# The last token blocks of an encoder layer get an order of their own, and every reciprocal root a third-order step

## The chip, the cores and the metric

The kernel runs on one core of one Trainium2 chip. The core has a matrix engine (TensorE, PE in the profile), a vector engine (VectorE, DVE), an activation engine (ScalarE, ACT), GpSimd (POOL) and a queue engine (SyncE, SP) that issues nearly all transfers between HBM and on-chip memory. Each engine carries out its instructions in the order in which they were written into its stream, and they wait for each other on semaphores. The metric is the device time of one execution in microseconds, lower is better.

## The reference, cut to what matters

One encoder layer is computed for two independent sequences of 512 tokens, `x_prompt` and `x_sample`, with 1024 channels:

```python
def rms_norm(x, g):
    xf = x.astype(jnp.float32)
    y = xf * lax.rsqrt(jnp.mean(xf * xf, axis=-1, keepdims=True) + EPS)
    return (y * g.astype(jnp.float32)).astype(x.dtype)

def swiglu(x, w_gate, w_up, w_down):
    return (jax.nn.silu(x @ w_gate) * (x @ w_up)) @ w_down

# encoder_layer: D_MODEL 1024, D_FF 2816
    x = x + 0.5 * swiglu(rms_norm(x, ffn1_norm), ffn1_w_gate, ffn1_w_up, ffn1_w_down)
    ...   # attention and a bidirectional mLSTM, side by side, merged and projected
    x = x + 0.5 * swiglu(rms_norm(x, ffn2_norm), ffn2_w_gate, ffn2_w_up, ffn2_w_down)
# trunk
    return rms_norm(x, final_norm)
```

The change touches the very end: the last additions into `x`, and the final `rms_norm`, which needs for each token the sum of squares over all 1024 channels before any of its channels can be scaled and stored. It also touches the reciprocal square root that every normalization in the layer uses.

## The kernel before, in words

**Stages.** The first feed-forward runs for both sequences together (profile lines L282 and L523), then the mixing stage (attention and mLSTM) once for each sequence (L678, L906, L932, L1013 and others), then the second feed-forward for both together, again L282 and L523. Each fp32 product is made of three matmuls on a high and a low part of the operands.

**The down projection.** `ffn_down` forms its 2x2 block product (two sequences by two halves of the channels) out of seven block products instead of eight; `DOWN` names them in the order in which they run, ending with T4, T1, B22. The 2816 hidden channels are taken in four chunks, so there are 28 steps, and the last seven finish the outputs. A step gives four token blocks of 128 tokens (`d` or `b`, 0 to 3), each a 128x512 tile in one PSUM bank. `flush_` adds the finished bank to its accumulator (L540). In the last seven steps it then calls `done(s, h, b)`: sequence `s`, half `h` of the channels, token block `b`. T4 finishes (0,1), T1 finishes (1,1), and B22, the last product of all, finishes (1,0). T1 and B22 use the same four banks (three named mm, one named pso), so B22's matmuls on a bank wait until T1's addition has read it.

**After each block.** `done2` squares the finished half on ScalarE with a running sum (`square`, L1152), and multiplies it in place by half of `final_norm` (L1338): on GpSimd, or on VectorE for (1,0). Once all halves of a group of token blocks are there (four blocks for sequence 0; blocks 0 and 1, then 2 and 3, for sequence 1), `row_scale` (L1161) adds the two half sums and runs `rstd_cols`, a chain of twelve small VectorE instructions (L157 to L168) that computes the reciprocal root from an integer first guess and three Newton steps. Then each block of 128x1024 is scaled by its root on ScalarE (L1352; the last block of sequence 1 on VectorE, L1350), and SP stores it with one 512 KB transfer (L1353).

**The order.** A planner orders each engine's instructions from the program's order, its priorities and its own estimate of costs. An instruction passed through `pin` (`tc.keep_in_program_order`) keeps its place in the program's order. In `done2` nothing is pinned. `rstd_cols` is used by 21 chains over the whole kernel, so an instruction more or less in it can change the planner's order elsewhere. Its small tiles come from a pool with five buffers for each width.

Of the kernel before, what the change touches and what calls it, by code (L numbers as in the profile page):

```python
# [16 lines left out]
P = 128  # L17
S = 512
D = 1024
# [3 lines left out]
EPS = 1e-6  # L23
# [3 lines left out]
def encoder(ctx, tc, I, outs):  # L27
    nc = tc.nc
# [5 lines left out]
    spool = ctx.enter_context(tc.tile_pool(name="spool", bufs=4))  # L34
# [7 lines left out]
    def nm(s):  # L42
        n_id[0] += 1
        return f"{s}_{n_id[0]}"
# [98 lines left out]
    def emit_hl(src, g, k, xh, xl):  # L143
# [2 lines left out]
                                       op0=ALU.mult, op1=ALU.subtract)  # L146
        return i1, i2

    def rstd_cols(v, width, n):


        def t_(dt=F32):
            w = max(width, 4)
            return spool.tile([P, w], dt, tag=f"rs{w}", bufs=5, name=nm("rs"))[:, 0:width]
        V = nc.vector
        a = t_()
        V.tensor_scalar(a, v, 1.0 / n, EPS, op0=ALU.mult, op1=ALU.add)  # L157
        b = t_(I32)
        V.tensor_scalar(b, a.bitcast(I32), 1, None, op0=ALU.logical_shift_right)
        y_ = t_(I32)  # L160
        V.tensor_scalar(y_, b, -1.0, 1597463007.0, op0=ALU.mult, op1=ALU.add)
        y = y_.bitcast(F32)
        for _ in range(3):
            t = t_()
            V.scalar_tensor_tensor(t, y, -0.5, y, op0=ALU.mult, op1=ALU.mult)
            V.tensor_tensor(t, t, a, op=ALU.mult)
            r = t_()
            V.scalar_tensor_tensor(r, t, 1.5, y, op0=ALU.add, op1=ALU.mult)  # L168
            y = r
        return y  # L170

    def col_sums(acc, bs=(0, 1, 2, 3)):
        p = PT()
# [42 lines left out]
    V_ = nc.vector  # L216
    G_ = nc.gpsimd
    HK_ = KD // 2

    B11, B21, B22, T4, T1, T2_, T3 = range(7)  # L220
# [215 lines left out]
    DH = KD // 2  # L436
    n_steps = len(DOWN) * len(CHUNKS)

    def ffn_down(wd, rb, ring, tail, xres, done, at_step, hook):
# [91 lines left out]
        def flush_(i, d, p):  # L531
            m, last = DOWN[i % 7], i >= n - 7
            acc = {B11: e16[:, d], T2_: e16[:, DH + d], T1: e5[:, d], B21: xs[0][:, d], T4: xs[0][:, DH + d],
                   T3: xs[1][:, DH + d], B22: xs[1][:, d]}[m]
            if last and m == T1:
                acc = xs[1][:, DH + d]
            if i < 7 and m in (B11, T2_, T1):
                nc.scalar.activation(acc, p, AF.Copy, scale=0.5)
            else:
                V_.scalar_tensor_tensor(acc, p, 0.5, acc, op0=ALU.mult, op1=ALU.add)  # L540
# [616 lines left out]
    def row_scale(sq, n=slice(0, 4)):  # L1157

        w = n.stop - n.start
        t = spool.tile([P, 4], F32, tag="cs4", bufs=4, name=nm("rsum"))[:, 0:w]  # L1160
        V_.tensor_tensor(t, sq[:, 0, n], sq[:, 1, n], op=ALU.add)  # L1161
        return rstd_cols(t, w, D)
# [86 lines left out]
    nhl = [None, None]  # L1249
    ssq1, ssq2, ssq3 = [[sums_tile() for _ in range(2)] for _ in range(3)]  # L1250

    def done1(s, h, b):
# [75 lines left out]
    fn = []  # L1328
# [3 lines left out]
        for half in range(2):  # L1332
            nc.gpsimd.dma_start(fn[half], I["final_norm"][half * S:(half + 1) * S].partition_broadcast(P))

    def done2(s, h, b):
        x_ = xs[s][:, h * 4 + b, :]
        square(x_, ssq3[s][:, h, b:b + 1])
        (V_ if (s, h) == (1, 0) else G_).tensor_tensor(x_, x_, fn[h], op=ALU.mult)  # L1338
        if s == 0 and h == 1 and b == 3:
            n = slice(0, 4)  # L1340
        elif s == 1 and h == 0 and b % 2:
            n = slice(b - 1, b + 1)
        else:
            return
        r = row_scale(ssq3[s], n)
        for i in range(n.start, n.stop):
            v = xs[s].rearrange("p (h b) c -> p h b c", h=2)[:, :, i, :]
            r_ = r[:, i - n.start:i - n.start + 1]
            if s and i == 3:
                V_.tensor_scalar(v, v, r_, None, op0=ALU.mult)  # L1350
            else:
                nc.scalar.activation(v, v, AF.Copy, scale=r_)  # L1352
            nc.sync.dma_start(outs[s][0, i * P:(i + 1) * P, :].rearrange("p (h c) -> p h c", h=2), v)  # L1353

    ffn_down(I["ffn2_w_down"][0], rbuf[1], up.ring, tail, lambda s, h: x2buf[s][:, h], done2, n_steps - 14, load_fn)


def host_consts():
# [39 lines left out]
```

## Time and profile before

| quantity | value |
|---|---|
| time, median of three runs | 2130.68 us (2130.02 to 2132.34) |
| time of the profiled execution | 2131.81 us |
| its span, first to last instruction | 2130.0 us |
| TensorE matmul busy | 2071.1 us, 97% of the span |
| VectorE busy | 1579.5 us, 74% |
| ScalarE busy | 968.5 us, 45% |
| GpSimd busy | 104.1 us, 5% |
| mean granted TensorE clock | 0.997 |

The profile is of one execution. Its rows give a start in microseconds from the span's start, a duration, the engine, the line of the kernel, the operation and the tiles; a bracket at the end names the idle time just ahead of an instruction and what ended it. A row with a count above 1 merges instructions that follow each other, and its duration is theirs together. VectorE and ScalarE let an independent instruction begin a little before the one ahead has ended, so start-to-start distances are shorter than durations.

### The profile page before, as it was taken

How to read it: one execution, taken by the hardware profiler on the slowest of the kernel's cores; microseconds unless marked ns; L12 is line 12 of the kernel's file. 1: busy time of each engine (PE TensorE's matmuls, PEld its weight loads, DVE VectorE, ACT ScalarE, POOL GpSimd, SP SyncE). 2: the span in 40 equal slices, each digit the busy share in tenths (PEclk: the TensorE clock that was granted, in tenths of full speed). 3: DMA queues.
4: the chain of work that ended last, by engine and by line, in shares of the span. 5: the costliest groups of instructions: out<-in, count | busy, mean ns of one | idle time of the engine just before them, and what ended most of it. 6: DMA issues, size and time to landing. Idle time of an engine off the chain costs nothing.

```text
span 2130.0 us, 26826 instructions
## 1 busy us (share of the span) xinstructions
PE 2071.1 (97%) x9472; PEld 1689.2 (79%) x9472; DVE 1579.5 (74%) x2817; ACT 968.5 (45%) x1739; POOL 104.1 (5%) x110
## 2 busy tenths in 40 slices
PE   6999999999999999999999999999999999999997
PEld 5877788888888777878887887788877778888885
DVE  7888887776696796574668755754978887786686
ACT  6534444442225466454435654544644444442223
POOL 1000000001000110100102001010000000000002
PEclk9999999999999999999999999999999999999998
DMA  8465554389765222333352232454464654479753
GB/s 266 150 197 186 182 196 142 131 303 378 281 219 162 78 71 64 95 103 97 117 159 81 60 90 79 129 178 158 154 197 159 197 165 166 142 261 386 284 207 122
DMA packets 294486, 361.81 MB, mean 170 GB/s; under 512 B 17776, under 2 KB 187776, under 8 KB 293328
## 3 DMA queue, kind: packets, MB, share of 16 engines
q1 hardware_dynamic: 293760, 358.84, 50.6%
q0 software_dynamic: 592, 1.27, 0.3%
q8 instruction: 74, 1.21, 0.2%
q14 instruction: 60, 0.49, 0.1%
HBM read 255.15 MB, written 104.89 MB: 169 GB/s over the span
## 4 chain that ended last, share of the span: by engine, by line
PE 74%; DVE 10%; DMA 6%; issue 6%; ACT 4%; POOL 0%; SPq 0%; DVEq 0%; ACTq 0%; POOLq 0%
PE mm L678 14%; PE pss L282 13%; PE pst L282 8%; PE mm L523 8%; PE mm L282 7%; PE pss L523 4%; PE pst L523 4%; PE mm L662 3%; PE pso L523 3%; DMA rbuf<-t 2%; DMA wr<-in_ffn_w_up_dram 2%; PE pso L932 1%; PE mm L1106 1%; PE pso L1062 1%; DVE w L241 1%
## 5 line engine op out<-in xcount | busy, mean ns | idle before, releaser
L678 PE MATMUL mm<-xh,w 128*128 128x512 f32 x896 | 292.0, 395 | 0.0
L282 PE MATMUL pss<-xc,w 128*128 128x512 f32 x1056 | 258.4, 391 | 12.4 <-DVE t L311 12.4
L282 PE MATMUL mm<-xc,w 128*128 128x512 f32 x1056 | 256.0, 391 | 2.5 <-ACT f L291 2.4
L282 PE MATMUL pst<-xc,w 128*128 128x512 f32 x1056 | 255.4, 390 | 0.0
L282 PEld LDWEIGHTS pss<-xc,w 128*128 128x128 f32 x1056 | 196.6, 188 | 60.4 <-DVE t L311 20.0
L282 PEld LDWEIGHTS mm<-xc,w 128*128 128x128 f32 x1056 | 196.8, 188 | 46.8 <-ACT f L291 6.6
L282 PEld LDWEIGHTS pst<-xc,w 128*128 128x128 f32 x1056 | 197.3, 188 | 43.2 <-ACT t L315 2.5
L203 DVE TENSOR_TENSOR w<-wr,w 128x1024 fp32r<-128x1024 f32 (+1 forms) x112 | 135.9, 1215 | 106.0 <-ACT w L202 100.7
L678 PEld LDWEIGHTS mm<-xh,w 128*128 128x128 f32 x896 | 167.6, 188 | 32.1
L523 PE MATMUL mm<-w,rt 128*128 128x512 f32 x792 | 185.6, 390 | 1.1 <-DMA rt<-rbuf 1.1
L678 PE MATMUL mm<-xl,w 128*128 128x512 f32 x448 | 176.7, 394 | 0.0
L523 PEld LDWEIGHTS mm<-w,rt 128*128 128x128 f32 x792 | 148.4, 188 | 32.5 <-DMA rt<-rbuf 1.8
L240 ACT ACTIVATE w<-t 128x512 fp32r<-128x512 f32 x176 | 107.0, 628 | 122.8 <-DVE t L266 42.0
L202 ACT ACTIVATE w<-wr 128x1024 fp32r<-128x1024 f32 (+1 forms) x112 | 114.4, 1028 | 99.4 <-PE mm L678 29.4
L241 DVE TENSOR_TENSOR w<-t,w 128x512 fp32r<-128x512 f32 x176 | 118.0, 689 | 44.5 <-ACT w L240 41.5
L282 PE MATMUL pss<-xc,f 128*128 128x512 f32 x528 | 128.4, 392 | 0.0
L282 PEld LDWEIGHTS pss<-xc,f 128*128 128x128 f32 x528 | 98.2, 188 | 23.6 <-DVE t L319 3.6
L580 ACT ACTIVATE w<-wr 128x512 fp32r<-128x512 f32 x72 | 44.6, 631 | 132.4 <-PE pso L523 64.3
L580 ACT ACTIVATE w<-t 128x512 fp32r<-128x512 f32 x82 | 51.6, 632 | 115.9 <-PE pst L523 47.3
L678 PEld LDWEIGHTS mm<-xl,w 128*128 128x128 f32 x448 | 84.3, 188 | 15.7
L523 PE MATMUL pss<-w,rt 128*128 128x512 f32 x396 | 94.0, 389 | 0.0
L523 PE MATMUL pst<-w,rt 128*128 128x512 f32 x396 | 93.7, 389 | 0.0
(316 smaller groups left out, 3644.4 us busy)
## 6 DMA issues: line engine op xcount, KB each, us to landing
rt<-rbuf SPq DMA_DIRECT2D x154, 512.0 KB, 5.8
wr<-in_w_in_dram SPq DMA_DIRECT2D x72, 512.0 KB, 3.6
wr<-in_ffn_w_gate_dram SPq DMA_DIRECT2D x56, 512.0 KB, 5.3
rbuf<-tab SPq DMA_DIRECT2D x90, 256.0 KB, 3.2
wr<-in_ffn_w_up_dram SPq DMA_DIRECT2D x44, 512.0 KB, 4.2
rbuf<-t SPq DMA_DIRECT2D x88, 256.0 KB, 3.5
rbuf<-f SPq DMA_DIRECT2D x66, 256.0 KB, 3.2
rbuf<-R SPq DMA_DIRECT2D x64, 256.0 KB, 3.5
```

Of the source, the lines that this page charges most:

```text
L202: pin(nc.scalar.activation(hi, raw, AF.Copy))
L203: pin(lo_eng.tensor_tensor(lo, raw, f(hi), op=ALU.subtract))
L240: pin(nc.scalar.activation(t[:, 0], src, AF.Copy))
L241: pin(V_.tensor_tensor(t[:, 1], src, f(t[:, 0]), op=ALU.subtract))
L282: nc.tensor.matmul(p, a[:, k, :], xt[:, b, k, :], start=(first and k == 0 and i == 0), stop=(k == HK_ - 1 and i == 2), skip_group_check=True)
L523: nc.tensor.matmul(p, r[:, b, d * P:(d + 1) * P], u[:, a, :], start=(first and q == 0 and k == 0), stop=(q == len(us) - 1 and k == 2), ski ...
L580: nc.scalar.activation(hi, src, AF.Copy)
L662: nc.tensor.matmul(p[b][:, :N], a[:, k, bs], w_[:, kl, :], start=(k == 0 and i == 0), stop=(k == KD - 1 and i == 2))
L678: nc.tensor.matmul(p, a[:, k, :], b, start=(k == 0 and i == 0), stop=(k == n - 1 and i == 2))
L932: nc.tensor.matmul(po, Vst[:, kv_, hk, :], w, start=(kv_ == 0 and i == 0), stop=(kv_ == 3 and i == 1))
L1062: nc.tensor.matmul(po, vm[:, a, t, hs_], b, start=(t == 0 and n == 0), stop=(t == 3 and n == 2))
L1106: nc.tensor.matmul(p[b], a[:, k, bs], w_[:, k - k0, :], start=(k == 0 and i == 0), stop=(k == KD - 1 and i == 2))
```

## The change

**The root.** `rstd_cols` is split: it forms `a = v/n + EPS`, and the new `rstd_of` does the rest, with the integer guess, one Newton step (three instructions), and one step of third order (five instructions). That is eleven instructions where there were twelve, and five small tiles a chain. It applies to every normalization of the kernel.

**T1 of sequence 1, half 1.** The product with `final_norm` moves from GpSimd to VectorE and is written to `e5`, which is free by then. After block 3 one VectorE instruction forms `half_ms` (`hm`), the half's sum of squares over 1024 plus EPS.

**B22, half 0.** `flush_` hands the block to `ends2`, all of whose instructions are pinned. Blocks 0 to 2: addition (VectorE), square (ScalarE), product with `final_norm` into `e16` (VectorE). After block 1 comes the root chain of blocks 0 and 1 (`last_scale(0)`), after block 2 the scaling of block 0 on ScalarE, each half by itself, each with a store of its own (256 KB). Block 3 is added in two column halves of 256; the first is squared on ScalarE, the second on VectorE, and that partial sum goes into `hm`. Then block 1 is scaled and stored by halves; then the chain of blocks 2 and 3 runs; then block 3's half 0 is scaled and multiplied by `final_norm` in one VectorE instruction, its half 1 on ScalarE, block 2's half 1 on VectorE and its half 0 on ScalarE, with four stores. Sequence 0 keeps its way.

```diff
+    def rs_tile(width, dt=F32):
+        w = max(width, 4)
+        return spool.tile([P, w], dt, tag=f"rs{w}", bufs=5, name=nm("rs"))[:, 0:width]
+
+    def rstd_of(a, width, pin=lambda i: i):
+
+        V = nc.vector
+        t_ = lambda dt=F32: rs_tile(width, dt)
+        b = t_(I32)
+        pin(V.tensor_scalar(b, a.bitcast(I32), 1, None, op0=ALU.logical_shift_right))
+        y_ = t_(I32)
+        pin(V.tensor_scalar(y_, b, -1.0, 1597463007.0, op0=ALU.mult, op1=ALU.add))
+        y = y_.bitcast(F32)
+        t = t_()
+        pin(V.scalar_tensor_tensor(t, y, -0.5, y, op0=ALU.mult, op1=ALU.mult))
+        pin(V.tensor_tensor(t, t, a, op=ALU.mult))
+        pin(V.scalar_tensor_tensor(t, t, 1.5, y, op0=ALU.add, op1=ALU.mult))
+        y, t, p, q = t, y, b.bitcast(F32), t_()
+        pin(V.tensor_tensor(t, y, y, op=ALU.mult))
+        pin(V.tensor_tensor(t, t, a, op=ALU.mult))
+        pin(V.tensor_scalar(p, t, 0.375, -1.25, op0=ALU.mult, op1=ALU.add))
+        pin(V.tensor_tensor(p, p, t, op=ALU.mult))
+        pin(V.scalar_tensor_tensor(q, p, 1.875, y, op0=ALU.add, op1=ALU.mult))
+        return q
+
     def rstd_cols(v, width, n):
-        for _ in range(3):
-            t = t_()
-            V.scalar_tensor_tensor(t, y, -0.5, y, op0=ALU.mult, op1=ALU.mult)
-            V.tensor_tensor(t, t, a, op=ALU.mult)
-            r = t_()
-            V.scalar_tensor_tensor(r, t, 1.5, y, op0=ALU.add, op1=ALU.mult)
-            y = r
-        return y
+        a = rs_tile(width)
+        nc.vector.tensor_scalar(a, v, 1.0 / n, EPS, op0=ALU.mult, op1=ALU.add)
+        return rstd_of(a, width)
...
             if last and m == T1:
                 acc = xs[1][:, DH + d]
+            if last and m == B22 and ends:
+                ends(d, p, acc, e16, e5)
+                return
...
-                done(1, 1, d)
+                done(1, 1, d, e5)
...
-    def done2(s, h, b):
+    half_ms = [None]
+
+    def store(s, i, h, v):
+        return nc.sync.dma_start(outs[s][0, i * P:(i + 1) * P, h * S:(h + 1) * S], v)
+
+    def done2(s, h, b, spare=None):
         x_ = xs[s][:, h * 4 + b, :]
         square(x_, ssq3[s][:, h, b:b + 1])
-        (V_ if (s, h) == (1, 0) else G_).tensor_tensor(x_, x_, fn[h], op=ALU.mult)
...
+        if s:
+            V_.tensor_tensor(spare[:, b], x_, fn[1], op=ALU.mult)
+            if b == 3:
+                t = half_ms[0] = spool.tile([P, 4], F32, tag="cs4", bufs=4, name=nm("hm"))
+                V_.tensor_scalar(t, ssq3[1][:, 1], 1.0 / D, EPS, op0=ALU.mult, op1=ALU.add)
             return
+        G_.tensor_tensor(x_, x_, fn[h], op=ALU.mult)
...
+    def last_scale(b0):
+
+        a = rs_tile(2)
+        sq, hm = ssq3[1][:, 0, b0:b0 + 2], half_ms[0][:, b0:b0 + 2]
+        pin(V_.scalar_tensor_tensor(a, sq, 1.0 / D, hm, op0=ALU.mult, op1=ALU.add))
+        return rstd_of(a, 2, pin)
+
+    first_r = []
+
+    def ends2(b, p, acc, pre0, pre1):
+
+        H = S // 2
+        ssq, hm = ssq3[1][:, 0, b:b + 1], half_ms[0][:, 3:4]
+        junk = T2(F32, "f2")
+
+        def on_act(i, h, r):
+            v = (pre0, pre1)[h][:, i]
+            pin(nc.scalar.activation(v, v, AF.Copy, scale=r))
+            pin(store(1, i, h, v))
+
+        if b < 3:
+            pin(V_.scalar_tensor_tensor(acc, p, 0.5, acc, op0=ALU.mult, op1=ALU.add))
+            pin(nc.scalar.activation(junk, acc, AF.Square, accum_out=ssq))
+            pin(V_.tensor_tensor(pre0[:, b], acc, fn[0], op=ALU.mult))
+            if b == 1:
+                first_r.append(last_scale(0))
+            if b == 2:
+                for h in range(2):
+                    on_act(0, h, first_r[0][:, 0:1])
+            return
+        for c in (slice(0, H), slice(H, S)):
+            pin(V_.scalar_tensor_tensor(acc[:, c], p[:, c], 0.5, acc[:, c], op0=ALU.mult, op1=ALU.add))
+            if c.start == 0:
+                pin(nc.scalar.activation(junk[:, c], acc[:, c], AF.Square, accum_out=ssq))
+        more = spool.tile([P, 4], F32, tag="cs4", bufs=4, name=nm("more"))[:, 0:1]
+        pin(V_.scalar_tensor_tensor(junk[:, H:], acc[:, H:], 1.0, acc[:, H:], op0=ALU.mult, op1=ALU.mult, accum_out=more))
+        pin(V_.scalar_tensor_tensor(hm, more, 1.0 / D, hm, op0=ALU.mult, op1=ALU.add))
+        for h in range(2):
+            on_act(1, h, first_r[0][:, 1:2])
+        r = last_scale(2)
+        pin(V_.scalar_tensor_tensor(acc, acc, r[:, 1:2], fn[0], op0=ALU.mult, op1=ALU.mult))
+        on_act(3, 1, r[:, 1:2])
+        pin(store(1, 3, 0, acc))
+        pin(V_.tensor_scalar(pre1[:, 2], pre1[:, 2], r[:, 0:1], None, op0=ALU.mult))
+        pin(store(1, 2, 1, pre1[:, 2]))
+        on_act(2, 0, r[:, 0:1])
```

More of the change, by code (lines that the diff above doesn't have):

```diff
@@ L437, in encoder, with ffn_down @@
     n_steps = len(DOWN) * len(CHUNKS)
-    def ffn_down(wd, rb, ring, tail, xres, done, at_step, hook):
+    def ffn_down(wd, rb, ring, tail, xres, done, at_step, hook, ends=None):
         n = n_steps
@@ L1355, in encoder @@
[L1355 removed]
+        if s:
[3 more added lines that the diff above has]
+                V_.tensor_scalar(t, ssq3[1][:, 1], 1.0 / D, EPS, op0=ALU.mult, op1=ALU.add)
+            return
+        G_.tensor_tensor(x_, x_, fn[h], op=ALU.mult)
+        if h == 0 or b < 3:
+            return
@@ new lines, in done2 @@
+        r = row_scale(ssq3[s])
+        for i in range(4):
+            v = xs[s].rearrange("p (h b) c -> p h b c", h=2)[:, :, i, :]
+            nc.scalar.activation(v, v, AF.Copy, scale=r[:, i:i + 1])
+            nc.sync.dma_start(outs[s][0, i * P:(i + 1) * P, :].rearrange("p (h c) -> p h c", h=2), v)
+    def last_scale(b0):
[3 more added lines that the diff above has]
+        return rstd_of(a, 2, pin)
@@ L1358, in host_consts @@
+    ffn_down(I["ffn2_w_down"][0], rbuf[1], up.ring, tail, lambda s, h: x2buf[s][:, h], done2, n_steps - 14, load_fn,
+             ends2)
 def host_consts():
```

26 lines of the change are left out of this document (2 added, 24 removed).

## The prediction

> **What bounds the kernel now.** I read the page's busy table first, then TensorE's waits over the whole span.
>
> ```profile
> PE 2071.1 (97%) x9472; PEld 1689.2 (79%) x9472; DVE 1579.5 (74%) x2817; ACT 968.5 (45%) x1739; POOL 104.1 (5%) x110
> PE pss L1147 <- DVE raw L1195: 13.7, 2, 11.3
> PE pst L848 <- DVE t L581: 4.4, 4, 1.8
> PE pst L185 <- DVE rs L168: 1.7, 4, 0.5
> ```
>
> TensorE is the bound: it idles for 2130.0 - 2071.1 = 58.9 us. What the change can win lies in that idle time, and most of it at two places, the first 16 us and the end. So the end comes next, in the timeline:
>
> ```profile
> 2100.86 1.16 DVE L157 TENSOR_SCALAR rs<-rsum 128x4 f32<-128x4 f32 x1
> 2102.06 0.17 DVE L159 TENSOR_SCALAR rs<-rs 128x4 int32<-128x4 int32 x1
> 2102.26 0.17 DVE L161 TENSOR_SCALAR rs<-rs 128x4 int32<-128x4 int32 x1
> 2102.34 0.69 DVE L540 SCALAR_TENSOR_TENSOR xs<-mm,xs 128x512 f32<-128x512 f32 x1
> 2104.11 1.14 DVE L165 SCALAR_TENSOR_TENSOR rs<-rs 128x4 f32<-128x4 f32 x1
> 2105.48 0.16 DVE L168 SCALAR_TENSOR_TENSOR rs<-rs,rs 128x4 f32<-128x4 f32 x1
> 2105.74 4.28 ACT L1352 ACTIVATE xs<-xs,rs 128x1024 f32<-128x1024 f32 x4 [1.90 <-DVE rs L168]
> 2107.08 6.28 PE L523 MATMUL mm<-w,rt 128*128 128x512 f32 x27
> 2109.32 0.69 DVE L540 SCALAR_TENSOR_TENSOR xs<-mm,xs 128x512 f32<-128x512 f32 x1 [1.35 <-PE mm L523]
> 2109.92 0.61 ACT L1152 ACTIVATE f<-xs 128x512 f32<-128x512 f32 x1
> 2110.53 0.61 ACT L1152 ACTIVATE f<-xs 128x512 f32<-128x512 f32 x1
> 2111.05 0.19 ACT L1152 ACTIVATION_READ_ACCUMULATOR f<-xs 128x1 f32 x1
> 2112.49 1.29 DVE L1338 TENSOR_TENSOR xs<-xs,tab 128x512 f32<-128x512 f32 x1 [2.48 <-ACT f L1152]
> 2113.20 2.20 PE L523 MATMUL pso<-w,rt 128*128 128x512 f32 x9
> 2118.26 0.69 DVE L540 SCALAR_TENSOR_TENSOR xs<-pso,xs 128x512 f32<-128x512 f32 x1
> 2120.40 0.15 DVE L1161 TENSOR_TENSOR rsum<-sqs 128x2 f32<-128x2 f32 x1
> 2122.84 0.16 DVE L168 SCALAR_TENSOR_TENSOR rs<-rs,rs 128x2 f32<-128x2 f32 x1
> 2123.10 1.15 ACT L1352 ACTIVATE xs<-xs,rs 128x1024 f32<-128x1024 f32 x1 [1.02 <-DVE rs L168]
> 2123.11 0.75 DVE L1350 TENSOR_SCALAR xs<-xs,rs 128x1024 f32<-128x1024 f32 x1
> 2124.27 1.20 SPq L1353 DMA_DIRECT2D out_dram<-xs  x2
> 2122.00:2122.50 0.50, 0.00 (x0) 0.00 (x0) 0.36 (x3) 0.08 (x1) 0.00 (x0) 0.50 0.44 172
> 2128.00:2128.50 0.50, 0.00 (x0) 0.00 (x0) 0.00 (x0) 0.00 (x0) 0.00 (x0) 0.50 0.48 172
> 2121.07 4.40 SPq L1353 DMA_DIRECT2D out_dram<-xs  x4
> ```
>
> The last matmul ends at 2115.40, and the span goes on for 14.6 us: VectorE and ScalarE alternate up to 2124.25, the last two stores follow. The last addition came at 2118.26, 2.9 us after its matmuls, since VectorE was held at 2112.49 by a square that stood on ScalarE behind four scalings, and worked off its backlog from there. The two window rows (last two figures: DMA share and GB/s) time the stores: the first of the last four was issued at 2121.07, and the share 0.44 of a half microsecond puts the first bytes at 2122.28, 1.21 later; the last bytes move until 2128.24. From there to 2130.0 are 1.76 us of completion and closing instructions, which the change leaves alone.
>
> **The change part by part: the end.** I follow the new instruction streams as built, with these steps: a small root instruction every 0.20 us (2102.06 to 2102.26); a 128x512 VectorE instruction 0.69 long, the next after 0.60 if independent (2102.34 to 2102.94 in the row's neighbours), after 0.71 if it reads the result; a ScalarE square 0.61 to the next, result 0.71 after its start (2110.53 to 2111.05 + 0.19); 0.1 from one engine's end to another's start. For halves and smaller stores:
>
> ```profile
> 901.38 0.42 DVE L1029 SCALAR_TENSOR_TENSOR t<-pss,t 128x256 f32<-128x256 f32 x1
> L580 ACT ACTIVATE w<-t 128x512 fp32r<-128x512 f32 x82 | 51.6, 632 | 115.9 <-PE pst L523 47.3
> L1216 SPq DMA_DIRECT2D xnbuf<-t x8: 319/329/632, 23.0 to 30.1; - x8
> xbuf<-xs SPq DMA_DIRECT2D x16, 256.0 KB, 2.0
> L1353 SPq DMA_DIRECT2D out_dram<-xs x8: 533/534/650, 2106.9 to 2124.9; - x8
> ```
>
> 1. *T1's products on VectorE.* Four instructions of 0.69 leave GpSimd. Two now stand inside sequence 0's root chain, with a second addition: 3 x 0.6 to 0.7 more there. The stall at 2104.11 (1.14 where its like takes 0.16) goes, for it ran beside a GpSimd product; that at 2100.86 stays, since T4's products stay on GpSimd. One chain instruction less: 0.2. From the addition at 2102.34 I count seven small steps, two products, one addition and the closing step: the chain ends at 2106.17, not 2105.64. The four scalings start at 2106.25, 0.5 late.
> 2. *The wait at `hm`.* It needs all four T1 squares. Two of them still stand on ScalarE behind the scalings, which take 4.18 us to the next square (2105.74 to 2109.92): squares at 2110.43 and 2111.04, the last result at 2111.75. `hm` runs at 2111.8, and queued behind it on VectorE is B22's first addition, which before ran at 2109.32. So VectorE loses 2.5 us there: the held place moves, it does not vanish. TensorE does not feel it, as T1 has freed the banks by then.
> 3. *B22, blocks 0 and 1.* Addition 2111.85, product to 2113.25, addition 2113.16, product to 2114.56; square of block 1 2113.94 to 2114.65. The chain (eleven instructions, 10 x 0.20 + 0.16) runs from 2114.7 to 2116.8.
> 4. *Blocks 2 and 3.* Addition of block 2 at 2116.74, product to 2118.14. Block 3 in halves at 2118.05 and 2118.39, each 0.42 (together 0.76 where one took 0.69); its second square on VectorE to 2119.25, `hm` to 2119.45. ScalarE: square of block 2 to 2118.23, two scalings of block 0 (0.55 start to start, 0.63 long) to 2119.3, half square to 2119.7. It comes last. Second chain 2119.73 to 2121.86; before it ended at 2122.84 + 0.16 = 2123.00. Win 1.14. Its last instruction also waits for block 1's two scalings (same small buffer), at 2120.8: hidden.
> 5. *Last scalings and stores.* Block 3 half 0 on VectorE to 2122.58, block 2 half 1 to 2123.0; ScalarE 2121.95 to 2122.55 and to 2123.1, against 2124.25. A piece of 512 columns is ready sooner than one of 1024, so SP issues the first of the last four at 2122.6, not 2124.27: 1.67 earlier. Four issues of 0.33 and a little wait end by 2124.2, faster than 256 KB move (2 x 512 KB took from 2125.50 to 2128.24, 0.69 a quarter), so transfer bounds them: 2122.6 + 1.21 + 2.74 = 2126.55, against 2128.24. Block 0 and 1's four stores, from 2118.9 on, are through by 2122.9.
>
> So the end wins 1.7 us. Bounds: nothing, or 0.1 lost by the halves, if ScalarE runs 1.7 later than I have it; 3.4 if the `hm` wait were not there (first addition at 2109.32 again, B22's chain then waiting for the squares).
>
> **The roots elsewhere.** One instruction less in 21 chains (63 rows of L165, three each). At the start the chains stand alone between the data and TensorE's first work, the 13.7 us wait, twice: 0.2 each, 0.4. At L185 TensorE waited for a root four times, 1.7 us in all: between 0 and 0.8, I take 0.4, the middle, as each wait (0.5 at most) exceeds 0.2 but the neighbours move too. The other chains run beside matmuls: nothing.
>
> **The order in the mixing stage.** The shorter chains make the planner reorder sequence 0's attention: of 9454 TensorE instructions the order differs between places 3135 and 3540, and a few around 4060 to 4310 and 5945 to 6200. Same work, other interleaving. Its stake:
>
> ```profile
> 700.00:800.00 100.00, 93.90 (x471) 74.31 (x470) 88.41 (x170) 57.98 (x118) 14.28 (x10) 1.00 0.25 70
> 1100.00:1200.00 100.00, 96.29 (x487) 76.80 (x486) 81.73 (x165) 57.72 (x120) 14.33 (x10) 1.00 0.31 90
> 720.00:730.00 10.00, 7.50 (x37) 5.71 (x35) 10.00 (x15) 4.33 (x9) 2.61 (x2) 1.00 0.32 82
> ```
>
> The first figures are length and TensorE busy time: 6.1 us idle in sequence 0's attention, 3.7 in sequence 1's, which is the same work in a third order. VectorE is full where TensorE waits. The new order's score matmuls span places 3195 to 3613, the old one's 3187 to 3613, and the vector work ahead of each wait is much alike. I take nothing; bounds: 2.4 won (the other sequence's idle), 6.1 lost (idle doubled).
>
> **Sum.** 1.7 + 0.4 + 0.4 + 0 = 2.5 us. Span 2130.0 - 2.5 = 2127.5. The profiled execution took 2131.81, 1.8 around its span, and lies 1.1 over the median 2130.68, so it becomes 2129.3 and the median 2128.2, or -0.12%.
>
> **Rivals.**
> - *The reorder helps.* Sequence 0's attention idles like sequence 1's: 2.4 more, 2125.8. For it: 1.8 us of waits at L848 that another interleaving avoided. Against: VectorE is the limit there, and its work shrinks by 0.4 us only. Beyond 0.2% from a further win of 1.8.
> - *The reorder hurts.* TensorE's idle time there doubles: 2128.2 + 6.1 = 2134.3, slower. It decides from 2.5 us of new idle time. For: VectorE has no slack. Against: the same tasks and the same two ends of the stage.
> - *The end does not deliver.* ScalarE, its work in a fixed order, holds the second chain as before; 1.7 is lost: 2129.9. For: the wait at `hm`; against: 1.1 us of margin in step 4.
> - *Small stores cost.* If each of the last four stores waited for the one ahead, it would take 2.0 us (the row of xbuf, 256 KB) each: 2122.6 + 8.0 = 2130.6, against last bytes at 2128.24: 2.4 lost instead of 1.7 won at the end, with 0.8 from the roots 2132.3, slower. Against it: the four at 2121.07 were issued within 4.40 us while each takes longer to land than to issue, and bytes flowed without a break from the first to the second. The Trainium skill, "DMA: Bandwidth & Descriptors", section "Rules for kernel authors", asks for transfers of at least 1 MiB for full bandwidth, which speaks against halving 512 KB; by its formula (about 2.0 us fixed plus bytes at 436 GB/s, there for GpSimd's path) a 256 KB store would take an estimated 2.6 us, and four in a row 10.4. This trace shows stores overlapping, so the fixed part should be paid once.
>
> **How the numbers follow.** Forecast 0.54, with its own range 2126.4 to 2130.0 (end 3.4 to 0.1 won, L185 0 to 0.8); reorder helps 0.25; reorder hurts 0.09; end does not deliver 0.09; small stores 0.03. No change is within 0.2%, about what a measurement of this kernel can tell: 2126.4 to 2134.9. Faster than that: most of the second case and the forecast's lower edge, 0.27. Slower: half of the third and a rest, 0.06. Same: 0.67. For eight in ten I go from 2124.9 (a helping reorder with the end a little better) to 2132.3 (small stores, or two thirds of the reorder's loss).
>
> **What would show it.** Right: first B22 addition near 2.5 us later after its matmuls than before; second chain ending about 6.5 us after the last matmul (before: 7.6); first of the last four issues 7.2 after it (before 8.9); tail 12.9 instead of 14.6. TensorE's idle time within 700 to 800 near 6. Wrong: the last four stores with gaps in the DMA share; a tail of over 14 or under 11.5; TensorE's idle time in attention changed by over 2 us.

## The result, and the profile after

The changed kernel takes 2126.64 us (median of 21 runs, 2122.51 to 2132.76) against 2130.03 us for the kernel before, run beside it (21 runs, 2125.83 to 2132.34). The ratio is 0.9983, with a 95% interval of 0.9976 to 0.999: 3.6 us less, between 5.1 and 2.1. Single executions of one kernel lie up to 6 us from its median (standard deviation 2.6), as much as the effect and more, so the places where time changed are read here from profiles as distances inside one execution. The main one is the **tail**, the end of the span less the end of the last matmul. Its worth shows in repeats: two profiles of one kernel gave 13.30 and 13.29, of another 10.88 and 10.86, of a third 9.96 and 9.98.

The profiled execution of the changed kernel took 2130.28 us, with a span of 2128.5; like that of before it lies above the median. From its page, the busy table:

```profile
PE 2075.3 (97%) x9472; PEld 1691.8 (79%) x9472; DVE 1578.4 (74%) x2803; ACT 969.1 (46%) x1742; POOL 103.0 (5%) x106
```

TensorE is idle for 2128.5 - 2075.3 = 53.2 us, against 58.9. Its busy time is 4.2 us longer than before for the same 9472 matmuls; over the fourteen profiles it lies anywhere from 2070.7 to 2078.6, which is one part of the scatter. The end, in the timeline of the changed kernel (start, duration, engine, line, operation, tiles):

```profile
2100.66 1.16 DVE L176 TENSOR_SCALAR rs<-rsum 128x4 f32<-128x4 f32 x1
...
2105.65 0.16 DVE L171 SCALAR_TENSOR_TENSOR rs<-rs,rs 128x4 f32<-128x4 f32 x1
...
2105.90 4.27 ACT L1365 ACTIVATE xs<-xs,rs 128x1024 f32<-128x1024 f32 x4
...
2111.43 0.17 DVE L1357 TENSOR_SCALAR hm<-sqs 128x4 f32<-128x4 f32 x1 [2.93 <-ACT f L1162]
2111.51 0.68 DVE L1389 SCALAR_TENSOR_TENSOR xs<-mm,xs 128x512 f32<-128x512 f32 x1
...
2113.00 2.20 PE L530 MATMUL pso<-w,rt 128*128 128x512 f32 x9
...
2114.37 0.16 DVE L1372 SCALAR_TENSOR_TENSOR rs<-sqs,hm 128x2 f32<-128x2 f32 x1
...
2116.43 0.68 DVE L1389 SCALAR_TENSOR_TENSOR xs<-mm,xs 128x512 f32<-128x512 f32 x1
...
2119.06 0.40 ACT L1401 ACTIVATE f<-xs 128x256 f32<-128x256 f32 x1
...
2119.59 0.16 DVE L1372 SCALAR_TENSOR_TENSOR rs<-sqs,hm 128x2 f32<-128x2 f32 x1 [0.42 <-ACT f L1401]
...
2121.64 0.16 DVE L171 SCALAR_TENSOR_TENSOR rs<-rs,rs 128x2 f32<-128x2 f32 x1
...
2121.84 0.75 DVE L1408 SCALAR_TENSOR_TENSOR xs<-xs,rs,tab 128x512 f32<-128x512 f32 x1
```

The last matmul ends at 2115.20. VectorE stands for 2.93 us at `hm`, until the last T1 square is back from ScalarE, and B22's first addition runs only then. From there VectorE is busy, but for 0.42 us ahead of the second chain, which ends at 2121.80. The first three of the last four stores in the timeline of the SP queue, and the end in windows (the last two figures are the DMA share and GB/s):

```profile
2122.58 0.33 SPq L1348 DMA_DIRECT2D out_dram<-e  x1
2123.01 0.38 SPq L1348 DMA_DIRECT2D out_dram<-xs  x1
2123.48 0.40 SPq L1348 DMA_DIRECT2D out_dram<-e  x1
...
2125.50:2126.00 0.50, 0.00 (x0) 0.00 (x0) 0.00 (x0) 0.00 (x0) 0.00 (x0) 0.50 0.97 369
2126.00:2126.50 0.50, 0.00 (x0) 0.00 (x0) 0.00 (x0) 0.00 (x0) 0.00 (x0) 0.50 0.40 148
2126.50:2127.00 0.50, 0.00 (x0) 0.00 (x0) 0.00 (x0) 0.00 (x0) 0.00 (x0) 0.50 0.06 25
```

Up to about 2126.2 the stores fill all sixteen transfer engines. Then a share of 0.06, which is one engine of sixteen, goes on for the whole next half microsecond, to 2127.05. What kept that engine is in the DMA view of the window 2124.7 to 2125.3 (queue, kind: packets, MB, share):

```profile
q1 hardware_dynamic: 122, 0.22, 100.0%
q14 instruction: 1, 0.01, 3.2%
```

One packet there is not data: a fetch of instructions, 8 KB by its 0.49 MB in 60 packets over the whole run. It took 0.31 us of one engine (3.2% of sixteen engines for 0.6 us), and one engine ended some 0.7 us behind the others. That the packet is the cause is tested in e10; why 0.7 us are lost to a packet of 0.31 stays open. All distances from the end of the last matmul, in us:

| event | before | forecast | after |
|---|---|---|---|
| second chain ends | 7.59 | 6.46 | 6.60 |
| first of the last four stores issued (before: of the last two, twice the size) | 8.87 | 7.2 | 7.38 |
| bulk of the bytes through | 12.83 | 11.15 | 11.1 |
| last byte through | 12.97 | 11.15 | 11.85 |
| from the last byte to the end of the span | 1.64 | 1.76 | 1.46 |
| span ends (the tail) | 14.61 | 12.9 | 13.30 |

The forecast took its 1.76 from the bulk of the bytes before (14.61 less 12.83, by the share of a window); the last transfer record of before ends 0.14 later, which leaves 1.64.

The roots elsewhere show in TensorE's idle time by stage (length of the window less busy time). Windows of before, then of after:

```profile
0.00:60.00 60.00, 43.77 (x204) 36.39 (x205) 46.66 (x105) 39.65 (x62) 5.50 (x12) 0.97 0.86 263
640.00:810.00 170.00, 163.66 (x841) 133.56 (x840) 138.77 (x286) 96.06 (x196) 15.61 (x20) 1.00 0.34 99
810.00:1000.00 190.00, 188.73 (x888) 151.85 (x887) 116.52 (x277) 99.85 (x199) 12.32 (x10) 1.00 0.32 94
1220.00:1400.00 180.00, 178.84 (x838) 144.04 (x836) 106.55 (x260) 92.85 (x185) 12.12 (x10) 1.00 0.34 100
```

```profile
0.00:60.00 60.00, 44.39 (x207) 37.21 (x208) 46.98 (x104) 40.19 (x63) 5.25 (x12) 0.97 0.87 268
640.00:810.00 170.00, 165.27 (x842) 135.08 (x841) 137.39 (x283) 96.59 (x197) 19.89 (x20) 0.99 0.33 99
810.00:1000.00 190.00, 189.01 (x887) 151.74 (x886) 116.38 (x270) 99.42 (x199) 12.40 (x10) 1.00 0.31 92
1220.00:1400.00 180.00, 179.08 (x837) 143.99 (x836) 106.13 (x254) 92.52 (x185) 12.11 (x10) 1.00 0.33 100
```

At the start the idle time falls from 16.23 to 15.61 (-0.6). In the two stretches with the mLSTM's root chains it falls from 1.27 + 1.16 = 2.43 to 0.99 + 0.92 = 1.91 (-0.5). In sequence 0's attention (640 to 810), where the planner's order is a new one, it falls from 6.34 to 4.73. The first two are terms of the prediction; whether the third belongs to the change is taken up below. With the tail they make 4.0 of the 5.7 us; the rest lies spread over the other stages, where two profiles of one kernel differ by more (45.3 and 42.7 us of idle time ahead of the last matmul in e7 and e12).

### The profile page after: what moved, and what is told of

It is laid out like the page before. It is cut to its first block, busy times and chain, and to the rows that moved or that the text cites. A ratio compares the mean times of both kernels' runs of the same rounds, so it can differ in the third digit from the quotient of the medians.

```text
span 2128.5 us, 26822 instructions
## 1 busy us (share of the span) xinstructions
PE 2075.3 (97%) x9472; PEld 1691.8 (79%) x9472; DVE 1578.4 (74%) x2803; ACT 969.1 (46%) x1742; POOL 103.0 (5%) x106
## 3 DMA queue, kind: packets, MB, share of 16 engines
q0 software_dynamic: 592, 1.27, 0.3%
q8 instruction: 74, 1.21, 0.2%
## 4 chain that ended last, share of the span: by engine, by line
PE 75%; DVE 9%; DMA 6%; issue 6%; ACT 4%; POOL 0%; SPq 0%; ACTq 0%; DVEq 0%; POOLq 0%
PE mm L688 14%; PE pss L289 14%; PE pst L289 8%; PE mm L530 8%; PE mm L289 7%; PE pss L530 4%; PE pst L530 4%; PE mm L672 3%; PE pso L530 3%; DMA rbuf<-t 2%; DMA wr<-in_ffn_w_up_dram 2%; PE pso L942 1%; PE mm L1116 1%; PE pss L916 1%; PE pso L1072 1%
```

## The experiments

The kernel before ran beside each group on the same chip: 2132.02 us beside the first four, 2131.16 beside the next four, 2132.34 beside the last four. Ratios are against it, with 95% intervals.

### Only the end: e1_end_only

The changed kernel, but `rstd_cols` keeps its three Newton steps; only the last two chains, which go through `last_scale`, have the new root. TensorE's order is that of before.

```
     def rstd_cols(v, width, n):
-        a = rs_tile(width)
-        nc.vector.tensor_scalar(a, v, 1.0 / n, EPS, op0=ALU.mult, op1=ALU.add)
-        return rstd_of(a, width)
+        ...
+        for _ in range(3):        # as in the kernel before
+        ...
```

> The end as changed, every other root chain with three Newton steps as before (sequence 0's last chain too). TensorE's order is that of the kernel before. My theory (the end earns what the profile shows, 14.6 us after the last matmul becoming 13.3; the rest of the measured 3.6 us comes from the roots elsewhere and the order they bring): tail 13.3 to 13.6, total 1 to 1.5 us under before. Rival (the end earns all): total 3 us or more under before.

Measured: 0.9993 (0.9983 to 1.0004), 1.5 us less, between 3.6 less and 0.9 more. The tail is 12.67, 1.94 shorter than before, and no instruction packet lies among its last stores. The idle time at the start (16.02) and in the mLSTM (2.41) is that of before. The tail is 0.6 shorter than expected, since the late engine of the changed kernel is missing. So the new end alone, when nothing disturbs its stores, is worth 1.9 us in the tail. By the idle time it isn't the whole gain; the times alone don't show that, as the rival's 3 us lie inside the interval.

### Only the roots: e2_roots_only

The kernel before with the new root in all 21 chains.

```
-        for _ in range(3):
-            ...
+        return rstd_of(a, width)
```

> The kernel before with the third-order root everywhere, its end otherwise unchanged. TensorE's order is that of the changed kernel. My theory: tail 14.2 to 14.6 (two chains of the end are shorter by 0.2 each), TensorE's idle time ahead of the last matmul 2 to 4 us less than before, total 1.5 to 2.5 us under before. Rival (the root does nothing outside the end): total within 0.5 us of before.

Measured: 0.9989 (0.998 to 0.9998), 2.3 us less, between 4.3 and 0.4. The tail is 14.15 (-0.46). The idle time is 15.41 at the start (-0.8) and 1.97 in the mLSTM (-0.5). TensorE's waits in this kernel (us in total, times, longest), where before had 13.7 and 1.7:

```profile
PE pss L1154 <- DVE raw L1202: 12.8, 2, 10.6
PE pst L192 <- DVE rs L171: 1.4, 4, 0.5
```

One small instruction less in each chain shows in just the two waits where a chain stands alone between data and matmuls. The tail, the start and the mLSTM add up to 1.7, within the measured interval. Ahead of the last matmul TensorE idles 3.4 us less (40.9 against 44.3), as expected, but half of that is sequence 0's attention (4.62 against 6.34), which has the changed kernel's order here too.

### More instructions in the root: e8_four_newton

The opposite: the kernel before with four Newton steps, three small instructions more in a chain.

```
-        for _ in range(3):
+        for _ in range(4):
```

> The kernel before with four Newton steps in every chain: three small instructions more instead of one less. My theory (the chains cost at the start, at L185 and in the end, 0.2 us an instruction): TensorE's first matmul of the products 0.6 us later, its idle time before the last matmul 2 to 4 us more, tail 15.4 to 15.8, total 3 to 5 us over before. Rival (chains cost in the end alone): total about 1 us over before.

Measured: 1.0008 (1.0 to 1.0017), 1.7 us more. Start 17.22 (+1.0), mLSTM 2.61 (+0.2), tail 15.39 (+0.8), together 2.0. The expectation failed in its size: 3 to 5 us more were forecast, and TensorE's idle time ahead of the last matmul is that of before (44.2 against 44.3), not 2 to 4 us more. The instructions cost where the chain stands alone, and nowhere else clear of the scatter; this kernel's order in attention is also a third one. Its wait at the start:

```profile
PE pss L1147 <- DVE raw L1195: 14.7, 2, 11.7
```

Three instructions more cost 1.0 there, one less saved 0.6 (the changed kernel) to 0.9 (e2). Single profiles differ by some tenths; over all of them the idle time of the first 60 us is 16.05 in the mean of the three with Newton's steps (before, e1, e5) and 15.59 in the mean of the ten with the new root. That is 0.46 for one instruction in the two chains together, against the 0.4 of the prediction.

### Without the wait at `hm`: e3_hm_late and e11_hm_late_again

`hm` is not formed behind the T1 products but just ahead of the first chain that needs it, behind the additions and products of B22's first two blocks. What needs neither `hm` nor the T1 squares then stands ahead of it.

```
@@ done2
             V_.tensor_tensor(spare[:, b], x_, fn[1], op=ALU.mult)
-            if b == 3:
-                t = half_ms[0] = spool.tile([P, 4], F32, tag="cs4", ...)
-                V_.tensor_scalar(t, ssq3[1][:, 1], 1.0 / D, EPS, op0=ALU.mult, op1=ALU.add)
             return
@@ ends2
             if b == 1:
+                t = half_ms[0] = spool.tile([P, 4], F32, tag="cs4", ...)
+                pin(V_.tensor_scalar(t, ssq3[1][:, 1], 1.0 / D, EPS, op0=ALU.mult, op1=ALU.add))
                 first_r.append(last_scale(0))
```

> The changed kernel with hm formed behind the additions and products of B22's blocks 0 and 1 instead of ahead of them. My theory (the wait at hm holds VectorE 2.4 us and delays everything behind it): first B22 addition at about 6.1 us ahead of the last matmul's end instead of 3.7, second chain and last store 1.6 us earlier, tail 11.7 instead of 13.3, total 1.6 us under the changed kernel. Rival (ScalarE's squares behind the four scalings hold the chain anyway): tail over 12.8.

Measured: 0.9959 (0.9946 to 0.9972), 8.7 us less; the tail is 10.88. The timeline of this kernel:

```profile
2105.89 0.69 DVE L1386 SCALAR_TENSOR_TENSOR xs<-mm,xs 128x512 f32<-128x512 f32 x1 [0.62 <-PE mm L530]
...
2107.93 0.69 DVE L1386 SCALAR_TENSOR_TENSOR xs<-mm,xs 128x512 f32<-128x512 f32 x1 [0.62 <-PE mm L530]
2107.99 0.19 ACT L1162 ACTIVATION_READ_ACCUMULATOR f<-xs 128x1 f32 x1
...
2109.26 0.18 ACT L1387 ACTIVATION_READ_ACCUMULATOR f<-xs 128x1 f32 x1
2109.27 0.16 DVE L1391 TENSOR_SCALAR hm<-sqs 128x4 f32<-128x4 f32 x1
2109.53 0.16 DVE L1369 SCALAR_TENSOR_TENSOR rs<-sqs,hm 128x2 f32<-128x2 f32 x1
...
2109.77 2.20 PE L530 MATMUL pso<-w,rt 128*128 128x512 f32 x9
...
2111.60 0.68 DVE L1386 SCALAR_TENSOR_TENSOR xs<-mm,xs 128x512 f32<-128x512 f32 x1
...
2114.76 0.16 DVE L1369 SCALAR_TENSOR_TENSOR rs<-sqs,hm 128x2 f32<-128x2 f32 x1 [0.42 <-ACT f L1400]
```

The first addition now waits for its matmuls (`PE mm`) and runs 6.08 us ahead of the last matmul's end (2111.97), where in the changed kernel it ran 3.69 ahead. `hm` itself is no earlier: it runs 2.70 ahead, where it ran 3.77 ahead, in its new place behind the product of block 1. It waits for nothing there, as the last T1 square is back at 2108.18. What holds the chain now is block 1: its addition waits 0.62 us for its matmuls, and its square, the fourth in a row on ScalarE, is back at 2109.44. The first chain starts at 2109.53, 2.44 ahead of the last matmul's end instead of 0.83, and the second 2.79 after it instead of 4.39. So 2.4 us at the first addition become 1.6 at both chains. Against a changed end without packet among its stores (12.47, in e6 and e10 below) the tail is 1.6 shorter. That it came out under the expected 11.7 is the late engine again, which this kernel doesn't have.

The 8.7 us are more than the tail's 2.4 against the changed kernel explains, with five runs only, so the same kernel ran again on the third chip.

> The kernel with hm formed late once more, beside the next: tail 10.9 as before; total, by its tail against the changed kernel's (2.4 shorter), 4.5 to 6 us under before, not the 8 of its first five executions, which I take for chance in good part.

Measured: 0.9975 (0.9965 to 0.9984), 5.3 us less, 12 runs; tail 10.86. The tail repeats to 0.02 and the time does not: 8.7 was partly the scatter of the executions ahead of the end. From the tail one expects 14.61 - 10.86 = 3.75, with the roots' 1.1 (0.6 at the start, 0.5 in the mLSTM) 4.9, which is what the second run gives.

### T1's products on GpSimd again: e4_t1_pool

```
-            V_.tensor_tensor(spare[:, b], x_, fn[1], op=ALU.mult)
+            G_.tensor_tensor(spare[:, b], x_, fn[1], op=ALU.mult)
```

> The changed kernel with T1's four products on GpSimd again. My theory (the move changed little: two products leave sequence 0's chain, but a chain instruction is stalled by about 1 us beside GpSimd): sequence 0's scalings start within 0.5 us of the changed kernel's, tail 13.0 to 13.8. Rival (the GpSimd products hold VectorE at each instruction): chain 1 us later or more, tail over 14.

Measured, one run: 2133.53 us; tail 12.74, no packet among the stores. Its timeline:

```profile
2106.37 1.29 POOL L1354 TENSOR_TENSOR e<-xs,tab 128x512 f32<-128x512 f32 x1 [1.10 <-DVE rs L163]
...
2106.39 1.28 DVE L164 TENSOR_TENSOR rs<-rs,rs 128x4 f32<-128x4 f32 x1
...
2115.10 0.17 DVE L1357 TENSOR_SCALAR hm<-sqs 128x4 f32<-128x4 f32 x1 [3.86 <-ACT f L1162]
```

A 128x4 step of the root chain takes 1.28 us, as long as the GpSimd product beside it, where its like take 0.16: the stall that the prediction saw at 2104.11 before, back again. Still the four scalings start 0.4 earlier, measured from the last matmul (9.72 ahead of its end against 9.30), since the products don't stand in the chain; and `hm` runs 0.2 later. The tail is 0.3 longer than the undisturbed 12.47, and under the 13.0 to 13.8 that were expected with a late engine. The move to VectorE is thus worth little, as steps 1 and 2 had it.

### 256 KB stores in the kernel before: e5_before_halfstores

```
-                nc.sync.dma_start(outs[s][0, i * P:(i + 1) * P, :].rearrange(...), v)
+            for h_ in range(2):
+                nc.sync.dma_start(outs[s][0, i * P:(i + 1) * P, h_ * S:(h_ + 1) * S], v[:, h_])
```

> The kernel before with each 512 KB output store issued as two of 256 KB. If small stores cost nothing beyond their issue (0.33 each instead of 0.53 for the pair's one): tail 14.4 to 14.8. Rival (each store pays its own fixed time in turn): tail over 16.

Measured, one run: 2136.14 us, with a mean granted clock of 0.991 against 0.997 in the profile of before, so the time says little; the tail is 14.21 against 14.61. The last eight stores in the SP queue, two windows, and the DMA view over all sixteen (KB each, median us to landing):

```profile
2125.79 5.00 SPq L1354 DMA_DIRECT2D out_dram<-xs  x8
...
2131.50:2132.00 0.50, 0.00 (x0) 0.00 (x0) 0.00 (x0) 0.00 (x0) 0.00 (x0) 0.50 0.98 385
2132.00:2132.50 0.50, 0.00 (x0) 0.00 (x0) 0.00 (x0) 0.00 (x0) 0.00 (x0) 0.50 0.98 389
...
out_dram<-xs SPq DMA_DIRECT2D x16, 256.0 KB, 2.4
```

Eight stores of 256 KB are issued in 5.0 us while each takes 2.4 to land, and the transfer engines are full at 385 GB/s to the end. Stores from one queue overlap, and halving them cost nothing; the tail is even 0.2 under the range expected for that.

### The old order in attention: e6_attention_newton

The changed kernel, with three Newton steps in the chains of width 8 and more, so that sequence 0's attention keeps TensorE's order of before.

```
     def rstd_cols(v, width, n):
+        if width >= 8:
+            return rstd_newton(v, width, n)     # as in the kernel before
```

> The changed kernel, with three Newton steps kept for the two kinds of attention chains (8 and 32 columns wide). TensorE's order in sequence 0's attention is then that of the kernel before, the rest that of the changed one. If the new order in attention helps: about 2 us over the changed kernel. If it does nothing (my forecast's reading): within 1 us of it.

Measured: 0.9991 (0.9982 to 1.0001), 1.9 us less, between 3.8 less and 0.2 more, beside 0.9989 for the changed kernel in the same group (next). That is 0.4 us over it by the ratios and 1.4 by the medians, so the time doesn't choose between the two expectations. The tail is 12.47: the instruction packet comes 7.76 us after the last matmul, ahead of the last four stores' bytes, and delays none of them. Sequence 0's attention in this kernel, and then in the changed kernel's second profile:

```profile
640.00:810.00 170.00, 164.91 (x848) 135.01 (x847) 138.31 (x289) 97.75 (x200) 18.98 (x20) 1.00 0.34 101
```

```profile
640.00:810.00 170.00, 166.52 (x858) 136.34 (x857) 136.71 (x286) 98.16 (x201) 14.88 (x20) 1.00 0.34 98
```

The idle time is 5.09 in the old order here, but 6.34 in before and 4.63 in e1, which have the same order. In the new order it is 3.48 here, 4.73 in the first profile, 4.62 in e2 and 5.37 in e7. Over all profiles one order scatters by 1.7 to 2.1 us, but the means differ: 5.45 in the four with the old order (before, e1, e5, e6), 4.21 in the nine with the new one, 1.2 less (0.3 to 2.2 at 95%). So the new one probably saves about 1 us in this stretch. The times, with intervals of 2 us to either side, don't settle whether the kernel keeps it, and as the old order always came with twelve-instruction chains, no run tells the order's part from theirs.

### Is the late engine chance? e9_after_again and e10_pad

I first took the instruction packet among the last stores for an accident of that execution. The changed kernel ran and was profiled again, unchanged.

> The changed kernel once more, unaltered, for its profile and time beside the others. My theory (one of the 16 transfer engines running 0.7 us late with its last rows was chance in the changed kernel's first profile): tail 12.6 instead of 13.3, last bytes on all transfer engines together, as the end-only kernel had it. Rival (storing by halves brings it about): last bytes late again, tail 13.2 or more.

Measured: 0.9989 (0.998 to 0.9997), 2.3 us less, between 4.3 and 0.6. The tail is 13.29, and the packet comes 9.66 us after the last matmul, as in the first profile. My theory of an accident fell. If the fetch depends on how far an engine has come in its stream, its place should move with the number of instructions. So the next kernel is the changed one with twelve small VectorE instructions at the very start, which write an unused tile:

```
+    pad = cpool.tile([P, 1], F32, name="pad")
+    for _ in range(12):
+        nc.vector.memset(pad, 0.0)
```

> The changed kernel with twelve one-column VectorE memsets of an unused tile at the very start, where VectorE waits for data; every other instruction and its order as in the changed kernel. My theory (an 8 KB instruction transfer, due at a fixed count of VectorE instructions, falls among the last four stores and makes one transfer engine late): the transfer comes 2 to 4 us earlier against the last matmul, ahead of the last four stores, and the tail is 12.5 to 12.7 instead of 13.3. Rival (it comes at its time whatever the count, or the stores themselves are uneven): tail 13.2 or more.

Measured: 0.9973 (0.9963 to 0.9983), 5.8 us less, between 7.9 and 3.6. The packet comes at 5.90 after the last matmul, 3.76 earlier, ahead of the last four stores; the DMA view of the window 2118.4 to 2119.0 and the windows at the end:

```profile
q1 hardware_dynamic: 99, 0.20, 91.4%
q14 instruction: 1, 0.01, 3.2%
...
2123.50:2124.00 0.50, 0.00 (x0) 0.00 (x0) 0.00 (x0) 0.00 (x0) 0.00 (x0) 0.50 0.18 62
2124.00:2124.50 0.50, 0.00 (x0) 0.00 (x0) 0.00 (x0) 0.00 (x0) 0.00 (x0) 0.50 0.00 0
```

After the half microsecond with the share 0.18 nothing moves any more: no engine lags, and the tail is 12.47, 0.83 shorter, though the kernel does more work. That the packet makes the lag is shown by this pair. How the place follows from the count is shown only roughly: with 3307 and 3389 VectorE instructions in the built program (e2, e8) no packet lay in the tail, with 3315 (after) it came at 9.66, with 3316 (e3) at 5.98, with 3326 (before) at 3.17, with 3331 (e1) at 0.63. More instructions mostly mean an earlier packet, but not strictly (3318 in e6 at 7.76, 3327 in e10 at 5.90); what triggers it was not measured.

### A shorter end: e7_more_end and e12_more_end_again

On top of e3: block 2 gets no product of its own (its scaling multiplies by `final_norm` in the same instruction), ScalarE scales half of block 0 ahead of block 2's square, and the half square of block 3 comes ahead of the other scalings.

```
@@ ends2, b < 3
+            accs.append(acc)
+            if b == 2:
+                on_act(0, 0, first_r[0][:, 0:1])
             pin(nc.scalar.activation(junk, acc, AF.Square, accum_out=ssq))
-            pin(V_.tensor_tensor(pre0[:, b], acc, fn[0], op=ALU.mult))
+            if b < 2:
+                pin(V_.tensor_tensor(pre0[:, b], acc, fn[0], op=ALU.mult))
...
-            if b == 2:
-                for h in range(2):
-                    on_act(0, h, first_r[0][:, 0:1])
@@ ends2, b == 3
-        for h in range(2):
-            on_act(1, h, first_r[0][:, 1:2])
+        for i, h in ((0, 1), (1, 0), (1, 1)):
+            on_act(i, h, first_r[0][:, i:i + 1])
...
-        pin(V_.tensor_scalar(pre1[:, 2], pre1[:, 2], r[:, 0:1], None, op0=ALU.mult))
-        pin(store(1, 2, 1, pre1[:, 2]))
-        on_act(2, 0, r[:, 0:1])
+        on_act(2, 1, r[:, 0:1])
+        pin(V_.scalar_tensor_tensor(accs[2], accs[2], r[:, 0:1], fn[0], op0=ALU.mult, op1=ALU.mult))
+        pin(store(1, 2, 0, accs[2]))
```

> The kernel with hm formed late, and besides: block 2 has no product with final_norm of its own (its scaling multiplies it in, as block 3's does), block 0's first half is scaled ahead of block 2's square, and the half square stands ahead of the other scalings. My theory (the second chain waits for VectorE's backlog and the half square): second chain 0.9 to 1.1 us earlier against the last matmul, tail 9.8 to 10.2 instead of 10.9. Rival (the stores of the first four pieces and the bandwidth bound the end by now): tail 10.5 or more.

Measured: 0.9974 (0.9965 to 0.9983), 5.5 us less; tail 9.96.

> The kernel with the shorter end once more, on the same chip as the one with hm formed late: tail 10.0, total 0.5 to 1.5 us under it if the end alone tells them apart; if its total is over that of the other, something ahead of the end differs.

Measured: 0.9967 (0.9955 to 0.9979), 7.0 us less, between 9.6 and 4.5; tail 9.98. The second chain's first instruction and the last block's addition, in the timeline of the second run:

```profile
2115.77 2.20 PE L530 MATMUL pso<-w,rt 128*128 128x512 f32 x9
...
2118.19 0.74 DVE L1399 SCALAR_TENSOR_TENSOR xs<-pso,xs 128x256 f32<-128x256 f32 x2
...
2119.70 0.16 DVE L1369 SCALAR_TENSOR_TENSOR rs<-sqs,hm 128x2 f32<-128x2 f32 x1
```

The chain starts 1.73 after the last matmul's end (2117.97), against 4.39 in the changed kernel and 2.79 in e3. This is the shortest end of all that ran, 4.6 us shorter than before and 3.3 shorter than the changed kernel's. In time it beats the kernel before; between it and e3 the times don't decide, the tail does (0.9).

## Why the prediction was right or wrong, point by point

**The forecast.** 2128.2 us was meant against a median of 2130.68, a gain of 2.5; the measured gain is 3.6 (5.1 to 2.1), and 2.3 (4.3 to 0.6) in the second group. Both intervals hold 2.5, and 2126.64 lies in the forecast's own range (2126.4 to 2130.0), close to its edge. By terms of the sum:

| term | forecast | shown by the rows |
|---|---|---|
| end | 1.7 | 1.3; without the late engine 1.9 to 2.1 (e1, e6, e10) |
| roots at the start | 0.4 | 0.6 (e2 0.8; means of all profiles 0.46; three instructions more in e8: 1.0) |
| roots in the mLSTM | 0.4 | 0.5 (e2 0.5; means of all profiles 0.45) |
| order in sequence 0's attention | 0 | 1.2 by the means of the window (0.3 to 2.2), not settled by the times |
| sum | 2.5 | 2.4 and what the order brings |

**Steps 1 and 2, the held place moves.** Right. Taking off 0.2 for the earlier last matmul, the scalings were forecast at 2106.05 and started at 2105.90; `hm` at 2111.6 against 2111.43. GpSimd's stall at the start of sequence 0's chain stayed, as the step said (1.16 us at 2100.66). B22's first addition ran 2.4 later against the last matmul (3.69 ahead of its end, before 6.08), near the 2.5 named as a sign. e3 shows that the wait at `hm` is what holds B22's additions.

**Steps 3 and 4, the chains.** Right within 0.2. The first chain starts 0.1 earlier than forecast after the shift; the second starts behind the half square on ScalarE, as the step has it, at 2119.59 against 2119.53, and ends 6.60 after the last matmul, against 6.46.

**Step 5, the stores.** This step failed in two points that partly hide each other. "Transfer bounds them: 2122.6 + 1.21 + 2.74 = 2126.55" holds for fifteen engines of sixteen: the bulk of the bytes was through after 11.1 us against 11.15. It took the bytes for all that the engines carry. The sixteenth had an instruction packet among its share and finished about 0.7 late, and the span waits for the last one. The other point is the 1.76 us from the last bytes to the end of the span, which the change was said to leave alone: they were 1.46 here, and 1.38 in e10, where no engine lags. So 0.7 too much and 0.3 too little make the tail 13.30 instead of 12.9; that it came so near is luck in part. e10 and e6, the same end with the packet elsewhere, have 12.47, 0.4 better than forecast, and 0.4 is what the closing is short of 1.76. The kernels with the old end (before, e2, e8, e5) close in 1.63 to 1.65, with 512 KB stores and with 256 KB stores alike; why the new end closes sooner was not found.

**The bound for the wait at `hm`.** It was said that without it the end would win 3.4. The rows of e3 and e11 give 14.61 - 10.87 = 3.74 in all, of which 1.6 come from taking away the wait, and an undisturbed end has 2.1 already. The size is right; as the step had it, the chain then waits for the squares, and in e3 as much for block 1's matmuls, which is why 2.4 us at the first addition are worth 1.6.

**The rivals.** *The reorder helps*: not refuted; it would have given 2.4 more, and the profiles speak for about half of that. The sign against it, idle time near 6 within 700 to 800, did not come: 4.7 and 3.4 in the two profiles of the changed kernel, the second more than 2 us off. The 6.1 of before was itself the highest of four profiles with the old order (4.5 to 6.1), so the term was read from one profile of a scattering stage. *The reorder hurts*: refuted, since the idle time in attention did not grow in any of the nine profiles with the new order (3.29 to 5.37, against 6.34 in before). *The end does not deliver*: refuted by e1's tail. *Small stores cost*: refuted by e5, where sixteen of them overlapped. On this point the Trainium skill, "DMA: Bandwidth & Descriptors", section "Rules for kernel authors", asks for transfers of at least 1 MiB for full bandwidth; here 256 KB stores, issued one behind the other, kept the engines at 385 GB/s, so the rule did not bind a run of overlapping stores in this case.

**The chances.** "Within 0.2%" was the likeliest and is what came, near its edge: the ratio 0.9983 lies inside, the interval reaches out to 0.9976. What the prediction left out was the scatter of the executions, which lies ahead of the end and is as large as the whole effect; the 1.1 us remainder between rows and measurement can't be told from it.

## What to carry to other kernels

An instruction on an in-order engine that waits for a slower engine should stand behind all work that doesn't need it: moving one 0.17 us instruction four places back was worth 1.6 us here, nearly as much as the whole rewritten end. A small instruction in a serial chain cost 0.2 us here wherever nothing else covered the chain, and nothing that could be seen elsewhere (e8), so its price is read from the waits and not from its count. Where an effect is as small as the scatter, measure it as a distance inside one profile, from the last matmul to the end, which repeated to 0.02 us when the times did not repeat to 3.

## What the runs showed of the hardware that was not expected

- Instruction fetches use the same transfer engines as data. One 8 KB packet of 0.31 us among the last stores made one engine of sixteen about 0.7 us late and the kernel's end with it (tail 13.30 and 13.29); twelve more instructions at the start moved it 3.76 us earlier and the tail to 12.47.
- Single executions scatter by 2 us and more at the same kernel, partly with the granted clock, which lay between 0.991 and 0.998, and partly without: the same 9472 matmuls kept TensorE busy for 2072.8 us in one profile with 0.993 (e1) and 2078.6 in another (e7).
- A 128x4 VectorE step that starts beside a running GpSimd product ends only with it: 1.28 us for 0.16 in e4 (ends at 2107.66 and 2107.67), 1.16 in the changed kernel (2101.82 and 2101.80). An addition out of PSUM was not held: it took its usual 0.69 at 2098.92 in the changed kernel, inside a GpSimd product from 2098.72 to 2100.01.
